# Two output gates moved between the value products of a linear attention, its heads' onsets spread, adaLN steps held around norms, context evictions moved ahead of splitting

## The chip, the cores and the metric

The kernel runs on one core of a Trainium2 chip. The metric is the time of one execution on the device, in microseconds (us); the median of three runs stands for a kernel.

## What is computed

Two transformer blocks run one after the other on 256 tokens of width 1024, in float32.

The first block has two layers. Each layer scales and shifts its input by vectors that come from a conditioning vector `c` (adaLN), runs a mixer (a bidirectional mLSTM and a dilated attention side by side), norms, and runs a SwiGLU:

```
ada = silu(c) @ w_ada[l] + b_ada[l]            # 6 vectors: sh1, sc1, g1, sh2, sc2, g2
u = h * (1 + sc1) + sh1
y = (sigmoid(g_a) * (mlstm(u) @ w_a) + sigmoid(g_b) * (attention(u) @ w_b)) @ w_out
h = layer_norm(ALPHA * h + g1 * y, ln1_g, ln1_b)
u = h * (1 + sc2) + sh2
h = layer_norm(ALPHA * h + g2 * swiglu(u), ln2_g, ln2_b)
```

The second block has two layers and a context of 256 more tokens. Layer 0 is a windowed attention with grouped keys over tokens and context, layer 1 a gated linear attention (GLA); both are followed by an MLP of width 4096 with a squared ReLU. Scales and shifts come from `silu(c) @ w_mod` in the same way, for tokens and for the context. GLA with four heads, in chunks of 64 positions and both directions, is cut to this:

```
q, k, v, out_gate = split(h @ w_in)
log_g = log_sigmoid(h @ gate_down @ gate_up + bias) / 16
b = cumsum(log_g)                       # within a chunk, and over the context
o = (tril((q*exp(b)) @ (k*exp(-b)).T)) @ v + (q*exp(b)) @ S      # S: state before the chunk
o = rms_norm(o, g_norm) * silu(out_gate)
x = x + m[2] * rms_norm(o @ w_o, g_post_mix)
```

## The kernel before, in words

**Granules.** All weights stream through the core once, as 591 granules of 512 KB (128 x 1024 floats) in one fixed list, `plan()` (line 34); 256 further granules hold the adaLN weights. A granule is named by a key such as `("gv", head, half)` or `("wo", layer, j)`. A float32 product is made of three faster matmuls: the weight is split in a high half `wh` (ACT, a rounded copy) and a low half `wl` (DVE, the difference), as the activations are, and each product is high x high, high x low, low x high.

**Ahead.** `gran(key, mm, post)` (line 483) first runs evictions that are due, then takes its granule with `G` (line 453). `G` calls `ahead(n)` (line 460), which issues the load of granule n+5 at most on SP (4 buffers `raw`), the high half of n+3 on ACT (4 buffers) and the low half of n+2 on DVE (3 buffers). So the `wl` of a granule is put into DVE's order two granules before PE uses it. Then `mm` issues the matmuls, and `post`, the eviction of the PSUM bank, is put off to the start of the next granule by `later(1, post)`. There are two PSUM buffers of name `mm`, four `aux`, two `trb`. Each engine runs its instructions in the order in which the program issues them.

**Ticks.** A granule ends with `tick()` (line 515): each generator in `self.bg` makes one step. Heads of attention, mLSTM and GLA are such generators: every step issues a few small instructions. `tick(False)` does the same without the adaLN step below. `until` and `drain` tick until a condition holds.

**adaLN steps.** `ada_step` (line 556) reduces one column block of adaLN weights against silu(c) on DVE: one pass of 128 x 1024, or two passes where tokens and context both need it (tile `junk`, then `araw`). It loads up to three blocks ahead into three `araw` buffers, counting its own. `tick` runs a step where `self.hold` is not set and the planner's lateness `nc.late` (line 372, DVE's planned time less PE's, in ns, with costs from lines 355 to 369) is below `self.room`, -250 in these stretches. `ada_need` forces the steps that are left of a vector; `affine` (line 850) needs the vectors 4 and 3 of its layer and then makes five small DVE instructions.

**layer1** (line 924) runs a layer of the first block. After the heads' projections come the branch gates `br` 0 to 7 (line 988), `wa` 0 to 7 (the products of the mLSTM's output), `wo` 0 to 7. For `wo`, `post` of an odd j makes `rT` of j-1 and j on DVE, and `trans` transposes `rT` of j-2 and j-1 on PE behind `wo` j (j even). `hold` is set after `wo` 7 and taken back at the end of `norm_to_u`. The norm is covered by filler granules of the context.

**Context.** `ctx_out` and `ctx_mlp` (lines 1727, 1758) are such fillers, in the feed-forward's end of layer 0 and of layer 1. Both use `nat` (line 1760), which multiplies two halves of four granules each and evicts two banks a half with ACT as `y` (line 1772). `relu2` and the norm's `u` and `ah` activations are on ACT too.

**GLA** (`layer2_gla`, line 1910). Granules in order: `gq`, `gg` 0 and 1 (output gates), `gdown`, four `gk`, eight `gv`, `gg` 2 to 7, then `gwo`. `decay()` runs in ticks beside `gk` and `gv`: softplus of the gate, a subtraction, and eight scans on DVE (line 1985). `head(hd, delay)` (line 2108) starts the two directions and the output of a head: exponentials on ACT, products and transposes of the decayed keys `ke`, states `gS`, the output `gon`, its norm, transposes, `go` (times the gate `og`) and the split `goT`. `bcast_cols` (line 1399) spreads a column vector over 128 rows with eight transposes into `trb` and two ACT copies.

Of the kernel before, what the change touches and what calls it, by code (L numbers as in the profile page):

```python
# [33 lines left out]
def plan():  # L34
# [95 lines left out]
    for h in range(4):  # L130
        for hf in range(2):
            g.append((("gv", h, hf), "gla_w_in_2", 0, "wsb", hf * 512, 1024 + h * 256))
    for j in range(2, 8):
        ws(("gg", j), "gla_w_in_2", 0, 2048 + j * 128)
# [242 lines left out]
class Kernel:  # L377
# [547 lines left out]
    def layer1(self, l, uT, ah, va, v1):  # L925
# [46 lines left out]
        for h in range(4):  # L972
# [13 lines left out]
            for j in range(2 * h, 2 * h + 2):  # L986
                self.gran(("o", l, j), self.mm_ws(ps[:, (j % 2) * 256:(j % 2) * 256 + 256], uT), post if j % 2 else None)
            for kind, j in EXTRA[h]:
                if l == 0 and h == 3 and (kind, j) == ("br", 6):
                    self.add(self.ctx_h())  # L990
# [28 lines left out]
        for j2 in range(4):  # L1019
            ps = self.mmb()  # L1020

            def post(j2=j2, ps=ps):
                t = self.t2("mtmp", (128, 2, 256))
                nc.vector.scalar_tensor_tensor(out=t, in0=sg(j2), scalar=1.0, in1=self.pair(ps), op0=ALU.add, op1=ALU.mult)
                nc.vector.tensor_tensor(out=t, in0=t, in1=mb.pair[j2], op=ALU.add)
                self.split(mt[j2][:, :, 0], mt[j2][:, :, 1], t)
            if j2 == 0:
                self.until(lambda: len(ydone) >= 3)
                self.first_ws([("wa", l, 0), ("wa", l, 1)], ps, lambda k: yaT[k], lambda: self.until(lambda: len(ydone) == 4))
                self.later(1, post)  # L1030
                if l:
                    self.add(self.ctx_u())
                continue
            for jj in range(2):
                self.gran(("wa", l, j2 * 2 + jj), self.mm_ws(ps[:, jj * 256:(jj + 1) * 256], yaT), post if jj == 1 else None)
# [6 lines left out]
        nc.vector.tensor_scalar(out=g1, in0=self.ada[l][:, 16:24], scalar1=0.5, scalar2=None, op0=ALU.mult)  # L1042
        cols = self.affine(l, 3, 4, (self.V(("ln1_g", l)), self.V(("ln1_b", l))))
        nat = [[None] * 2 for _ in range(2)]
# [12 lines left out]
        for j in range(8):  # L1057
# [15 lines left out]
            if j > 0 and j % 2 == 0:  # L1073
                trans(j - 2)
                trans(j - 1)
            if j == 6:
                stats(0)
# [649 lines left out]
    def ctx_out(self):  # L1727
# [3 lines left out]
        self.yc = self.halves(y)  # L1731
        yield from self.nat(lambda hf, kp: ("awo", 1, hf, kp), self.tokens(oT), self.yc, self.mmb)

# [18 lines left out]
    def ctx_mlp(self):  # L1752
        y = [self.t4("y", (128, 1024)) for _ in range(2)]
        self.yc = self.halves(y)
        yield from self.mlp_out(0, 1, self.hid_c, self.yc, self.mmb)
        self.hid_c = []
        yield from self.mlp_in(1, 1, self.uc, self.hid_c)
        self.flush()

    def nat(self, key, act, y, bank, add=False):  # L1760

        nc = self.nc
        for hf in range(2):
# [9 lines left out]
            for kp in range(4):  # L1773
                self.gran(key(hf, kp), self.mm_nat(kp, act, banks), post if kp == 3 else None)
                yield True
# [11 lines left out]

    def mlp_out(self, g, st, hid, y, bank):

        return self.nat(lambda hf, kp: ("mo", 0, g, hf, kp, st), hid if callable(hid) else self.tokens(hid), y, bank, g > 0)  # L1790

# [118 lines left out]
    def layer2_gla(self, x, xc):  # L1910
# [5 lines left out]
        for hd in range(4):  # L1916
            ps = self.mmb()
            self.grans2(("gq", hd), self.mm_ws(ps[:, 0:256], hl),
                        lambda hd=hd, ps=ps: nc.scalar.activation(out=qT[:, hd], in_=ps[:, 0:256], func=AF.Copy, scale=128 ** -0.5))
        bank = [None]  # L1920

        def gates(j0, j1, gran):

            for j in range(j0, j1):
# [4 lines left out]
                def post(j=j, ps=ps):  # L1929
                    th = self.t2("gth", (128, 2, 256))  # L1930
                    nc.scalar.activation(out=th, in_=self.pair(ps), func=AF.Tanh, scale=0.5)
                    nc.vector.scalar_tensor_tensor(out=og.pair[j // 2], in0=th, scalar=1.0, in1=self.pair(ps), op0=ALU.add, op1=ALU.mult)
                gran(("gg", j), self.mm_ws(ps[:, (j % 2) * 256:(j % 2) * 256 + 256], hl), post if j % 2 else None)
        gates(0, 2, self.grans2)
# [21 lines left out]
        def decay():  # L1956
# [33 lines left out]
            ldone.append(1)  # L1990
        self.add(decay())
        kT = [self.tv("gkT", (128, 2, 512)) for _ in range(2)]
        for hd in range(4):
            ps = self.mmb()
            self.gran(("gk", hd), self.mm_ws2(ps, h), lambda hd=hd, ps=ps: nc.scalar.activation(out=kT[hd // 2][:, hd % 2], in_=ps, func=AF.Copy))
            if hd:
                self.tick(False)
        v = [None] * 4
        ss = self.small([128, 2, 4], "gss", 1)
# [61 lines left out]
        def outputs(hd):  # L2061
# [28 lines left out]
            for jj in range(2):  # L2090
                for b in range(2):
                    nc.tensor.transpose(tr[:, jj * 256 + b * 128:jj * 256 + b * 128 + 128], on[:, b, jj * 128:(jj + 1) * 128], self.ident)
            yield
            o32 = self.t2("go32", (128, 2, 256))
            for jj in range(2):
# [17 lines left out]
        def values(hd):  # L2113
# [19 lines left out]
            for hf in range(2):  # L2133
                self.gran(("gv", hd, hf), mm(hf))
                steps(2)
        while self.adaq:
            self.ada_step()
        gmix = self.gain_cols(1, "g_post_mix_2", 2, 0)
        cols = self.scales(1, "g_pre_mlp_2", 3, 4, (0,))
        for hd in range(4):  # L2140
            if hd == 1:
                self.until(lambda: ldone)
                head(0, 1)
            if hd == 3:
                head(1, 1)
            values(hd)
        self.flush()
        head(2, 0)
        head(3, 5)
        oT = Lazy(lambda k: ot[k // 2][:, k % 2])  # L2150
        G = self.bcast_cols(gmix, "G")
        for j in range(2, 8):
            gates(j, j + 1, self.gran)
# [102 lines left out]
```

## Time and profile before

| | us |
|---|---|
| median of 3 runs (lowest, highest) | 2083.51 (2081.5, 2088.59) |
| profiled execution | 2092.44 |
| its span | 2090.7 |
| PE busy in it | 2030.9 (97%) |
| DVE, ACT busy | 1586.6 (76%), 1149.3 (55%) |
| mean DMA rate | 203 GB/s |

The span is the time from the first to the last instruction that the trace shows. PE is TensorE's matmuls, PEld its weight loads, DVE is VectorE, ACT is ScalarE, SP issues the DMAs. In a row of the timeline, the bracket gives the time for which the engine stood idle ahead of the instruction, and the instruction or transfer that ended that idle time. A weight load precedes its matmul, so the idle time of PEld is some tenths of a us longer than that of PE.

### The profile page before, as it was taken

The page shows a single profiled execution, that of the slowest core. Times are in us where ns is not written, and L with a number is a line of the kernel's source. Part 1 is how long each engine was busy: PE and PEld are TensorE (multiplying, and loading weights), DVE is VectorE, ACT ScalarE, POOL GpSimd, SP SyncE. Part 2 cuts the span into 40 slices and gives each one's busy share as a digit, 9 for nine tenths or more (in the row PEclk, how much of TensorE's full clock was granted, in tenths as well). Part 3 has the DMA queues.
Part 4 walks back from the last instruction along what each step waited for, and adds up shares of the span by engine and source line. Part 5 has one row for each costly group of instructions (what it writes and reads, how often), then busy time and mean ns, then how long its engine had stood idle before and what let it go on. Part 6 is the DMA issues. An engine that isn't in the chain of part 4 may idle for free.

```text
span 2090.7 us, 38245 instructions
## 1 busy us (share of the span) xinstructions
PE 2030.9 (97%) x15176; PEld 1888.9 (90%) x15176; DVE 1586.6 (76%) x2717; ACT 1149.3 (55%) x1968; POOL 45.1 (2%) x63
## 2 busy tenths in 40 slices
PE   7999999999999999998999999999999999999998
PEld 6999998899998989998999988899998989877997
DVE  7788988799978989988899776777563485466555
ACT  5756665655546656665744455556542464445444
POOL 0000000000000000000000000000000010000000
PEclk9999999999999999999999999999999999999999
DMA  9786566598876886555589755115553352214553
GB/s 340 281 320 213 192 235 221 187 315 305 304 254 228 284 274 233 187 202 186 167 290 358 274 196 176 61 56 176 191 183 101 115 181 75 77 65 155 188 191 132
DMA packets 120884, 426.88 MB, mean 204 GB/s; under 512 B 13664, under 2 KB 18528, under 8 KB 120704
## 3 DMA queue, kind: packets, MB, share of 16 engines
q1 hardware_dynamic: 120704, 424.43, 59.1%
q8 instruction: 119, 1.95, 0.4%
q14 instruction: 61, 0.50, 0.1%
HBM read 423.33 MB, written 1.05 MB: 203 GB/s over the span
## 4 chain that ended last, share of the span: by engine, by line
PE 87%; DVE 7%; ACT 4%; issue 1%; DMA 1%; POOL 0%; DVEq 0%; POOLq 0%; SPq 0%; ACTq 0%
PE mm L338 54%; PE aux L338 28%; PE trb L338 5%; DVE wl L338 1%; ACT wh L471 1%; DVE yg L338 1%; POOL rs L674 0%; ACT xh L1467 0%; DVE mtmp L338 0%; DMA raw<-in_w 0%; DVE xh L338 0%; DVE x L338 0%; DVE araw L338 0%; ACT ah L912 0%; DVE ee L338 0%
## 5 line engine op out<-in xcount | busy, mean ns | idle before, releaser
L338 DVE TENSOR_TENSOR wl<-raw,wh 128x1024 fp32r<-128x1024 f32 x591 | 718.7, 1221 | 153.1 <-PE aux L338 71.5
L471 ACT ACTIVATE wh<-raw 128x1024 fp32r<-128x1024 f32 x591 | 623.6, 1059 | 336.2 <-PE mm L338 117.7
L338 PE MATMUL mm<-uT,wh 128*128 128x256 f32 x3488 | 622.3, 282 | 0.0
L338 PEld LDWEIGHTS mm<-uT,wh 128*128 128x128 f32 x3488 | 531.7, 188 | 2.2 <-ACT va L814 0.3
L338 PE MATMUL mm<-uT,wl 128*128 128x256 f32 x1744 | 487.0, 279 | 0.0
L338 PE MATMUL mm<-hT,wh 128*128 128x256 f32 x1888 | 339.4, 283 | 4.8 <-ACT y L1772 2.1
L338 PEld LDWEIGHTS mm<-uT,wl 128*128 128x128 f32 x1744 | 329.6, 189 | 0.0
L338 PEld LDWEIGHTS mm<-hT,wh 128*128 128x128 f32 x1888 | 292.7, 190 | 11.5 <-ACT y L1772 2.3
L338 PE MATMUL mm<-hT,wl 128*128 128x256 f32 x944 | 265.8, 282 | 0.0
L338 DVE CUSTOM_DVE_ANT_0 araw<-araw,silu 128x1024 f32<-128x1024 f32 x192 | 233.2, 1220 | 8.4 <-DMA araw<-in_w 5.9
L338 PE MATMUL aux<-wh,hid 128*128 128x512 f32 x640 | 199.9, 394 | 0.0
L338 PEld LDWEIGHTS mm<-hT,wl 128*128 128x128 f32 x944 | 181.4, 192 | 0.0
L338 PEld LDWEIGHTS aux<-wh,hid 128*128 128x128 f32 x640 | 117.7, 188 | 23.6 <-DVE hid L338 0.2
L338 DVE TENSOR_TENSOR r<-r 128x256 f32<-128x256 f32 (+1 forms) x88 | 39.5, 448 | 117.4 <-ACT r L1905 117.3
L338 PE MATMUL aux<-mlg,wh 128*128 128x256 f32 x704 | 127.1, 283 | 0.0
L338 PE MATMUL aux<-wl,hid 128*128 128x512 f32 x320 | 124.8, 390 | 0.0
L338 PEld LDWEIGHTS aux<-mlg,wh 128*128 128x128 f32 x704 | 107.3, 188 | 0.0
L1905 ACT ACTIVATE r<-mm 128x256 f32<-128x256 f32 (+1 forms) x88 | 35.7, 406 | 125.1 <-PE mm L338 125.1
L338 PE MATMUL aux<-mlg,wl 128*128 128x256 f32 x352 | 98.8, 281 | 0.0
L674 POOL TENSOR_TENSOR rs<-ve,mhalf 128x1 f32<-128x1 f32 (+1 forms) x48 | 41.8, 871 | 2040.5 <-DVE ve L338 1853.0
L338 DVE CUSTOM_DVE_ANT_0 junk<-araw,silu 128x1024 bf16<-128x1024 f32 x64 | 77.9, 1218 | 0.0
L338 PE MATMUL mm<-wh,hT 128*128 128x256 f32 (+1 forms) x352 | 76.8, 316 | 0.6 <-DVE qs L338 0.6
(365 smaller groups left out, 3081.7 us busy)
## 6 DMA issues: line engine op xcount, KB each, us to landing
raw<-in_w SPq DMA_DIRECT2D x591, 512.0 KB, 3.9
araw<-in_w SPq DMA_DIRECT2D x192, 512.0 KB, 5.2
abias<-in_abias SPq DMA_DIRECT2D x32, 192.0 KB, 5.6
xc<-in_ctx SPq DMA_DIRECT2D x4, 512.0 KB, 6.1
x<-in_x SPq DMA_DIRECT2D x2, 512.0 KB, 4.2
gb<-in_ln SPq DMA_DIRECT2D x2, 512.0 KB, 5.4
out_x<-x SPq DMA_DIRECT2D x4, 256.0 KB, 2.0
mk<-in_mmask SPq DMA_DIRECT2D x1, 512.0 KB, 5.9
```

Source lines behind the costliest of these rows:

```text
L338: return f(*a, **k)
L471: nc.scalar.activation(out=wh, in_=self.raws[self.nhi], func=AF.Copy)
L674: nc.gpsimd.tensor_tensor(out=rs, in0=ve, in1=self.mhalf[:, 0:n], op=ALU.pow)
L1905: nc.scalar.activation(out=r[:, 0:n], in_=ps, func=AF.Relu)
```

## The change

Four parts:

1. GLA. `gg` 2 and 3 move in the plan from behind all value granules to between the two value granules of head 0 and those of head 1, each with one tick more. The heads start at other points: head 0 without delay behind the values of head 0, head 1 behind those of head 1 with a delay of 2, head 2 behind those of head 2 with 4, head 3 behind those of head 3 with 3; before, heads 0 and 1 started behind the values of heads 0 and 2 with a delay of 1, heads 2 and 3 behind those of head 3 with 0 and 5. The gain's columns and scales are made ahead of `gk`, and the broadcast `G` after the third `gk`. Four gate granules are left behind the values. A head waits for its gate before it multiplies with it (`gdone`).
2. In layer 0 and 1, `hold` is set ahead of `br` 3 of the last head. In layer 0 it is taken back after `wa` 1, in layer 1 it stays until the end of the norm.
3. `affine` of the first norm moves from ahead of `wo` 0 to behind the granule `wo` 3.
4. `nat` gets `prompt`: the eviction of a half is issued right behind the last product of that half, ahead of the next granule's splits. `ctx_out` and `ctx_mlp` use it.

```diff
@@ plan
-    for j in range(2, 8):
+        for j in (2, 3) if h == 0 else ():
+            ws(("gg", j), "gla_w_in_2", 0, 2048 + j * 128)
+    for j in range(4, 8):
         ws(("gg", j), "gla_w_in_2", 0, 2048 + j * 128)
@@ layer1
             for kind, j in EXTRA[h]:
+                if h == 3 and (kind, j) == ("br", 3):
+                    self.hold = True
...
                 if l:
                     self.add(self.ctx_u())
+                self.hold = l == 1
                 continue
...
-        cols = self.affine(l, 3, 4, (self.V(("ln1_g", l)), self.V(("ln1_b", l))))
...
                 trans(j - 1)
+            if j == 3:
+                cols = self.affine(l, 3, 4, (self.V(("ln1_g", l)), self.V(("ln1_b", l))))
@@ ctx_out, ctx_mlp: prompt=True; nat
-                self.gran(key(hf, kp), self.mm_nat(kp, act, banks), post if kp == 3 else None)
+                mm = self.mm_nat(kp, act, banks)
+                if kp == 3 and prompt:
+                    self.gran(key(hf, kp), lambda wh, wl: (mm(wh, wl), post()))
+                else:
+                    self.gran(key(hf, kp), mm, post if kp == 3 else None)
@@ layer2_gla
         self.add(decay())
+        while self.adaq:
+            self.ada_step()
+        gmix = self.gain_cols(1, "g_post_mix_2", 2, 0)
+        cols = self.scales(1, "g_pre_mlp_2", 3, 4, (0,))
...
             if hd:
                 self.tick(False)
+            if hd == 2:
+                G = self.bcast_cols(gmix, "G")
...
+            while hd not in gdone:
+                yield
             o32 = self.t2("go32", (128, 2, 256))
...
-        while self.adaq:
-            self.ada_step()
-        gmix = self.gain_cols(1, "g_post_mix_2", 2, 0)
-        cols = self.scales(1, "g_pre_mlp_2", 3, 4, (0,))
         for hd in range(4):
             if hd == 1:
                 self.until(lambda: ldone)
-                head(0, 1)
+                head(0, 0)
+            if hd == 2:
+                head(1, 2)
             if hd == 3:
-                head(1, 1)
+                head(2, 4)
             values(hd)
+            if hd == 0:
+                self.flush()
+                for j in (2, 3):
+                    gates(j, j + 1, self.gran)
+                    self.tick(False)
         self.flush()
-        head(2, 0)
-        head(3, 5)
+        head(3, 3)
         oT = Lazy(lambda k: ot[k // 2][:, k % 2])
-        G = self.bcast_cols(gmix, "G")
-        for j in range(2, 8):
+        for j in range(4, 8):
             gates(j, j + 1, self.gran)
             steps(2)
```

## Rows read from the trace of the kernel before

**Rows 1.** Page: busy share by engine; chain that ended last; adaLN's reduction group.

```profile
PE 2030.9 (97%) x15176; PEld 1888.9 (90%) x15176; DVE 1586.6 (76%) x2717; ACT 1149.3 (55%) x1968; POOL 45.1 (2%) x63
...
PE 87%; DVE 7%; ACT 4%; issue 1%; DMA 1%; POOL 0%; DVEq 0%; POOLq 0%; SPq 0%; ACTq 0%
...
L338 DVE CUSTOM_DVE_ANT_0 araw<-araw,silu 128x1024 f32<-128x1024 f32 x192 | 233.2, 1220 | 8.4 <-DMA araw<-in_w 5.9
```

**Rows 2.** Windows: us, busy time and (xinstructions) by engine, granted clock, DMA share, GB/s.

```profile
1249.00:1255.00 6.00, 4.64 (x26) 4.65 (x27) 3.22 (x5) 2.73 (x5) 0.00 (x0) 0.72 0.53 173
1776.00:1783.00 7.00, 4.15 (x22) 3.75 (x21) 4.68 (x12) 6.87 (x16) 0.00 (x0) 0.76 0.43 150
350.00:360.00 10.00, 7.60 (x67) 7.40 (x66) 8.06 (x18) 3.92 (x4) 0.00 (x0) 1.00 0.83 282
1753.85:1776.00 22.15, 22.15 (x194) 22.00 (x192) 18.62 (x22) 11.92 (x14) 0.00 (x0) 1.00 0.15 48
```

**Rows 3.** Timeline, DVE, GLA decay: start, us, engine line op, out<-in, count [idle <-releaser].

```profile
1765.83 9.03 DVE L338 TENSOR_TENSOR_SCAN ee<-reset,lg 128x512 f32<-128x512 f32 x8
1774.78 1.20 DVE L338 TENSOR_TENSOR wl<-raw,wh 128x1024 fp32r<-128x1024 f32 x1
```

**Rows 4.** Timeline, PE weight loads in GLA that waited [idle <-releaser].

```profile
1779.00 0.42 PEld L338 LDWEIGHTS trb<-ident,ke 128*128 128x128 f32 x4 [3.04 <-DVE ke L338]
...
1816.74 0.41 PEld L338 LDWEIGHTS trb<-ident,qgc 128*128 128x128 f32 x4 [1.50 <-ACT gkn L2039]
...
1818.07 0.30 PEld L338 LDWEIGHTS trb<-ident,qgc 128*128 128x128 f32 x3 [0.93 <-ACT G L1407]
...
1831.05 0.30 PEld L338 LDWEIGHTS aux<-gv,gkn 128*128 128x128 f32 x2 [1.42 <-ACT wh L471]
...
1866.08 0.30 PEld L338 LDWEIGHTS aux<-gv,ATm 128*128 128x128 f32 x2 [0.86 <-DVE ATm L338]
```

**Rows 5.** Timeline, DVE, the last head's output.

```profile
1870.37 0.42 DVE L338 COPY gon<-aux 128x256 f32<-128x256 f32 x1 [0.98 <-PE aux L338]
...
1873.28 0.62 DVE L338 TENSOR_SCALAR gon<-gon,rs 128x256 f32<-128x256 f32 x2 [0.81 <-POOL rs L674]
...
1878.77 0.69 DVE L338 TENSOR_TENSOR goT<-go,goT 128x512 fp32r<-128x512 f32 x1 [0.70 <-ACT goT L657]
```

**Rows 6.** Timeline, ACT, the last head's output.

```profile
1876.51 0.84 ACT L2096 ACTIVATE go<-trb,ggn 128x256 f32<-128x256 f32 x2 [2.36 <-PE trb L338]
1878.10 0.63 ACT L657 ACTIVATE goT<-go 128x512 fp32r<-128x512 f32 x1 [0.76 <-DVE go L338]
```

**Rows 7.** Timeline, DVE, around the output projection of layer 0.

```profile
349.10 1.22 DVE L338 CUSTOM_DVE_ANT_0 araw<-araw,silu 128x1024 f32<-128x1024 f32 x1
...
355.15 2.35 DVE L338 TENSOR_TENSOR wl<-raw,wh 128x1024 fp32r<-128x1024 f32 x2
359.37 0.88 DVE L338 SCALAR_TENSOR_TENSOR rT<-mm,g,ah 128x256 f32<-128x256 f32 x2 [1.87 <-PE mm L338]
```

**Rows 8.** Tile araw, 300 to 372 us: issue to landing of its loads.

```profile
DMA to landing us min/median/max: 3.1/4.3/8.0
```

**Rows 9.** Timeline, PE weight loads, output projection of layer 0.

```profile
353.37 0.19 PEld L338 LDWEIGHTS mm<-mT,wl 128*128 128x128 f32 x1 [2.60 <-DVE wl L338]
```

**Rows 10.** Timeline, DVE, layer 1: first pass of a double step.

```profile
944.70 1.20 DVE L338 CUSTOM_DVE_ANT_0 junk<-araw,silu 128x1024 bf16<-128x1024 f32 x1
```

**Rows 11.** Timeline, PE weight loads, layer 1.

```profile
951.23 0.14 PEld L338 LDWEIGHTS trb<-ident,mh 128*128 128x128 f32 x1 [2.11 <-ACT mh L1378]
...
977.67 0.19 PEld L338 LDWEIGHTS mm<-mT,wl 128*128 128x128 f32 x1 [2.22 <-DVE wl L338]
```

**Rows 12.** Timeline, ACT, the first eviction of ctx_mlp.

```profile
1249.70 1.09 ACT L1772 ACTIVATE y<-mm 128x512 f32<-128x512 f32 x2
```

**Rows 13.** Timeline, PE weight loads, context stages.

```profile
654.94 0.19 PEld L338 LDWEIGHTS mm<-wh,uT 128*128 128x128 f32 x1 [0.97 <-ACT y L1772]
...
1250.35 0.27 PEld L338 LDWEIGHTS mm<-hT,wh 128*128 128x128 f32 x1 [2.31 <-ACT y L1772]
```

More of the change, by code (lines that the diff above doesn't have):

```diff
@@ L1731, in ctx_out @@
         self.yc = self.halves(y)
-        yield from self.nat(lambda hf, kp: ("awo", 1, hf, kp), self.tokens(oT), self.yc, self.mmb)
+        yield from self.nat(lambda hf, kp: ("awo", 1, hf, kp), self.tokens(oT), self.yc, self.mmb, prompt=True)
     def ctx_u(self):
@@ L1754, in ctx_mlp @@
         self.yc = self.halves(y)
-        yield from self.mlp_out(0, 1, self.hid_c, self.yc, self.mmb)
+        yield from self.mlp_out(0, 1, self.hid_c, self.yc, self.mmb, True)
         self.hid_c = []
@@ L1758, in ctx_mlp, with nat @@
         self.flush()
-    def nat(self, key, act, y, bank, add=False):
+    def nat(self, key, act, y, bank, add=False, prompt=False):
         nc = self.nc
@@ L1786, in mlp_in, with mlp_out @@
             yield True
-    def mlp_out(self, g, st, hid, y, bank):
-        return self.nat(lambda hf, kp: ("mo", 0, g, hf, kp, st), hid if callable(hid) else self.tokens(hid), y, bank, g > 0)
+    def mlp_out(self, g, st, hid, y, bank, prompt=False):
+        return self.nat(lambda hf, kp: ("mo", 0, g, hf, kp, st), hid if callable(hid) else self.tokens(hid), y, bank, g > 0, prompt)
     def tokens(self, a):
@@ L1919, in layer2_gla @@
                         lambda hd=hd, ps=ps: nc.scalar.activation(out=qT[:, hd], in_=ps[:, 0:256], func=AF.Copy, scale=128 ** -0.5))
-        bank = [None]
+        bank, gdone = [None], []
         def gates(j0, j1, gran):
@@ L1932, in post @@
                     nc.vector.scalar_tensor_tensor(out=og.pair[j // 2], in0=th, scalar=1.0, in1=self.pair(ps), op0=ALU.add, op1=ALU.mult)
+                    gdone.append(j // 2)
                 gran(("gg", j), self.mm_ws(ps[:, (j % 2) * 256:(j % 2) * 256 + 256], hl), post if j % 2 else None)
```

## The prediction, before any run of the changed kernel

> **What bounds the kernel now.** I read the page first. TensorE (PE) is busy 97% of the span, and 87% of the chain that ended last is PE work, with 7% on DVE [rows 1]. The change removes no product and no pass: the same matmuls run in another order. So a part is worth only the PE idle time that it removes or makes, plus the clock that such idle time costs, and DVE, ACT and the DMA queues matter only where PE waits for them. Next I read PE's waits and weight loads, to list the gaps near the edits. The gaps that the edits can reach are 3.04 us in the gated linear attention (GLA), two at the broadcast of a gain, several under 1.5 us between its heads [rows 4], 2.60 in the output projection of layer 0 [rows 9], 2.11 and 2.22 in layer 1 [rows 11], 2.31 and 0.97 at context evictions [rows 13]. That is all there is to win: about 19 us, under 1% of the span.
>
> Two stretches carry a mean granted clock of 0.72 over 6 us and 0.76 over 7 us; a third, with an idle time as long, keeps 1.00 [rows 2]. At levels of 2.4 and 1.2 GHz the first two mean some 3.4 us at 1.2 GHz, which loses half of its work: **1.7 us**. A gap of 2.3 or 3.0 us brought this, one of 2.6 did not, so I treat the 1.7 as likely after a long gap and possible after a short one.
>
> **Part 1, GLA.** (a) Two gate granules now run between the value granules of head 0 and of head 1. PE's 3.04 us gap is a wait for decayed keys (`ke`), behind eight scans on DVE that take 9.03 us, 1765.83 to 1774.86 [rows 3, 4]. After the change these transposes come some 5.5 us later in PE's order and are not late. But the planner emits the low half `wl` two granules ahead. Today `wl` of gv(1,0) stands ahead of the scans and `wl` of gv(2,0) right behind them (1774.78, 1.20 us) [rows 3]. With two granules inserted, the one behind the scans is gv(1,0)'s own. 192 products (four value granules) take 22.15 us less a tail, 5.5 each [rows 2]. So PE reaches gv(1,0) at 1753.9 + 2 x 5.5 + 2 x 2.8 = 1770.5, or 1771.4 with the broadcast's eight transposes in front. DVE ends the scans at about 1775.8 and that `wl` at 1777.0. New gap: some 5.3 us; old gap 3.0, with the same clock slice. **+2.3**, between -1 (if the scans can start earlier) and +4. Queued behind the scans on DVE are also the gate's eviction and the next `wl`; PE then has 5.5 us of gv(1,0) to cover both.
> (b) The broadcast of the gain moves from after the value granules to the key granules, where ACT has free time. Its two gaps are 1.50 and 0.93 [rows 4]: **-2.3**.
> (c) Heads start at 0, 8, 16, 21 steps after the values of head 0, where it was 1, 13, 18, 23, with more product granules between their small steps. Six gaps stand there, the first 1.42, the last 0.86 [rows 4], 4.0 in all by PE's own starts. No row shows the new order, so I bound it from -3.6 to +1.5 and take **-1.8**, about half.
> (d) Only four gate granules (two fewer, 5.6 us) stand behind the heads, with two steps each, so head 3 finishes at its 40th step, when PE already wants its output as the fourth granule of `gwo`. The chain from output to split: 1870.37 to 1873.90, some 3.5 us [rows 5], is covered by one granule (2.8). Then transposes, the scaled eviction at 1876.51, the high half at 1878.10 [rows 6] and the low half until 1879.46 [rows 5], 2.2 to 2.95 us, with no product behind. Today two more granules cover both. **+3.7**, from 0 to +5.4 with a slice of slow clock. Part 1: **+1.9**, range -4 to +6.
>
> **Part 2, adaLN held back, layer 0.** The hold from br 3 to the second granule of `wa` skips six adaLN steps. Played through the planner's own figures, its lateness then stays above the -250 limit at each tick of wa 2 to wo 1, because the context's queue work fills DVE; one step is taken at wo 2, one at wo 3, and `affine`, moved to j = 3, then forces the other six. Gain: today two forced steps (349.10, 1.22 us each) and the affine stand ahead of two `wl` [rows 7], for which PE waits 2.60 [rows 9]; that goes, and about 0.7 in the chain of head 3: -3.3.
> Loss: what is queued behind the forced burst on DVE is `rT` of wo 2 and 3 (the eviction of j = 3 is run when wo 4 starts), and PE's transposes behind wo 4 wait for `rT`. Today PE has wo 3 done by 359.3, when that `rT` starts [rows 7]; 2.5 us earlier and with wo 4 (2.8) behind, PE asks at about 359.7. DVE is done with `wl` of wo 5 at 357.5 today [rows 7], at about 355.9 after. Seven steps at 1.15 (start to start) are 8.0, bias, affine and the first `rT` 1.2: 365.1, if no step waits, a gap of 5.4. But `araw` has three buffers and each step frees the one for the load three steps on; those loads land 3.1 to 8.0 us after issue, median 4.3 [rows 8]. With 4.1 the fourth, fifth, seventh and eighth steps end at 359.9, 362.3, 365.2 and 367.6 and the first `rT` at 368.8: a gap of **9.1 us**, bounds 5.4 and 11. I take 9.1, as these landings are in the same stretch. PE at rest that long should bring slow clock after it: +1.7, from 0 to 3.4. Layer 0: -3.3 + 9.1 + 1.7 = **+7.5**, from +2 to +11.
> Here the Trainium skill speaks against the change: "DMA: Bandwidth & Descriptors", Rules for kernel authors, says to issue a DMA early and wait for it late, so that its fixed cost overlaps; a burst over three buffers does the opposite. The page's fit (Anatomy of one DMA, made on the GpSimd path, 2.0 us + bytes / 436 GB/s) gives an estimate of 3.2 us for 512 KB, by which two rounds of waiting would be 1.8 us shorter, the gap 7.3 and the sum 1.8 us lower; the landings of this trace have a median of 4.3 and decide.
>
> **Part 3, layer 1.** Here four double steps (two passes, 944.70 being one, 1.20 each and 2.45 with overlaps [rows 10]) are held until the norm is done; nothing is forced, since layer 1's shifts were complete, and they go to the feed-forward stage, where DVE has room. The gap of 2.11 at 951.23 waits for a chain whose `mh` stood behind the step of 944.70: -1.9. The gap of 2.22 at 977.67 waits for a `wl` in a DVE queue that is 2.45 shorter: -2.2 [rows 11]. The affine's small operations before wo 0 move away: -0.5; the split of `mT` keeps its own wait: -0.3. **-4.9**, from -2.9 to -5.5. If the cover in the feed-forward stage is missing, each step costs up to 2.45 there; no PE gap in that stage waits for DVE today.
>
> **Part 4, evictions ahead of splitting.** `prompt` runs the eviction of a half right behind its last product instead of one granule later. In `ctx_mlp` the `y` copies (1249.70) stand behind four `u` activations [rows 12], and PE waits 2.31 for the banks [rows 13], with the slow slice of 1.7. Ahead of those activations the copies end before PE asks: **-3.9**, from -1 (if the next wait is the splitting itself, now 1.1 us later) to -4. In `ctx_out` the gap of 0.97 [rows 13] shrinks, but the copies go ahead of activations on which later `wl` and the norm wait: **+0.2**, from -0.7 to +1.
>
> **Sum.** 1.9 + 7.5 - 4.9 - 3.7 = **+0.8 us**. The profiled execution took 2092.4 us (span 2090.7, some 2 us around it), 9 us over the median of 2083.5; the gaps are set by order within the core, so I carry the sum over unchanged: 2093.2 for that execution, **2084.3** for the median. About 0.3%, 6.25 us, is what a measurement of this kernel can tell from no change.
>
> **Rivals.** (i) *Forecast*: layer 0 gives back what layer 1 and the context win: 2084.3, own range 2078 to 2090.
> (ii) *The burst wins, slower*: one mechanism, six forced steps behind three load buffers. If the landings are at the long end (one 8.0 us landing adds 4) and the slow clock lasts two slices (3.4), layer 0 is +12 to +13; with the tail of GLA at +5.4 the sum is +7 to +10: 2091 to 2095. It decides from a gap of about 13 us with its clock, at wo 4. For it: the median landing is already above what a gap of 9 needs. Against: SP carries fewer loads in that stretch, since weights wait too.
> (iii) *The steps do not burst, faster*: DVE reaches the burst early or its loads are ahead, so that the gap is under 3 us, and (a) is hidden: layer 0 -1, GLA -1.5, sum about -10: 2073 to 2076. For it: DVE is relieved of 6 x 1.2 = 7.2 us ahead of wo 0. Against: the planner counts PE's and DVE's time, not gaps, and by its figures starts only two.
> (iv) *It does little where it aims*: PE's next wait (the split of `mT`, the `u` activations) ends at the same time, layer 1 and the context give -3 together, and the burst is at 5.4: within 3 us of the forecast.
>
> **Chances.** Forecast 0.40, (iv) 0.17, (ii) 0.24, (iii) 0.19. The range takes in (iii)'s upper half and most of (ii): 2073 to 2095. Faster by over 0.3%: (iii) and a little of the others, 0.21. Slower: (ii) and the upper end of the forecast, 0.25. Within: 0.54.
>
> **What would show it.** Right: a new PE gap of 5 to 11 us near 360, waiting for `rT`, with eight `araw` reductions close together ahead of it and half clock behind; gaps at 353, 951, 977 and 1250 gone, 1250's slow slice too; a gap near 1772 that waits for `wl`; gaps before and inside the last granules of `gwo` waiting for `gon` and `goT`; none at the broadcast. Wrong: `araw` steps spread over wa 2 to wo 1, a gap at 360 under 4 us, no gap near 1772, or new gaps in the feed-forward stage of layer 1 behind the deferred steps. The sum hangs above all on the 9.1.

## The result, and the profile after

The changed kernel takes 2101.2 us (median of 5 runs, 2096.58 to 2102.81) against 2088.59 us for the kernel before, measured beside it again (5 runs, 2081.5 to 2090.83). The ratio is **1.0061, with a 95% interval of 1.0040 to 1.0082**: 8 to 17 us slower. The forecast was 2084.3, no change that can be told, with a range that ended at 2095. Of the 16.9 us between forecast and result, 5.1 are the base, which the forecast took from three runs (2083.51); 11.8 are the change, +12.6 where the sum said +0.8.

The page of the changed kernel, profiled execution of 2096.58 us (span 2094.8), shares of engines and the chain that ended last:

```profile
PE 2022.7 (97%) x15176; PEld 1879.4 (90%) x15176; DVE 1585.9 (76%) x2717; ACT 1149.3 (55%) x1968; POOL 45.5 (2%) x63
...
PE 85%; DVE 7%; ACT 4%; issue 2%; DMA 1%; POOL 1%; DVEq 0%; POOLq 0%; SPq 0%; ACTq 0%
```

As many products as in [rows 1], and 2 points less of the chain on PE. PE is idle 72.1 us of the span, 59.8 before: 12.3 us more. That it is busy 8.2 us less, although more of its products ran at the lower clock, goes with a faster pace of PE in this execution, to which the last section comes. The largest piece of the idle time lies where the forecast put it. DVE from wo 2 to the third `rT` of layer 0 (start, us, then the instruction; in brackets the idle time before it and what ended that):

```profile
353.02 0.87 DVE L340 SCALAR_TENSOR_TENSOR rT<-mm,g,ah 128x256 f32<-128x256 f32 x2
...
354.94 1.22 DVE L340 CUSTOM_DVE_ANT_0 araw<-araw,silu 128x1024 f32<-128x1024 f32 x1
...
357.22 1.22 DVE L340 CUSTOM_DVE_ANT_0 araw<-araw,silu 128x1024 f32<-128x1024 f32 x1
...
359.81 1.23 DVE L340 CUSTOM_DVE_ANT_0 araw<-araw,silu 128x1024 f32<-128x1024 f32 x1 [1.37 <-DMA araw<-in_w]
...
362.47 1.23 DVE L340 CUSTOM_DVE_ANT_0 araw<-araw,silu 128x1024 f32<-128x1024 f32 x1 [1.42 <-DMA araw<-in_w]
...
364.32 1.22 DVE L340 CUSTOM_DVE_ANT_0 araw<-araw,silu 128x1024 f32<-128x1024 f32 x1 [0.62 <-DMA araw<-in_w]
...
365.58 1.23 DVE L340 CUSTOM_DVE_ANT_0 araw<-araw,silu 128x1024 f32<-128x1024 f32 x1
...
368.02 1.23 DVE L340 CUSTOM_DVE_ANT_0 araw<-araw,silu 128x1024 f32<-128x1024 f32 x1 [1.20 <-DMA araw<-in_w]
...
369.24 1.23 DVE L340 CUSTOM_DVE_ANT_0 araw<-araw,silu 128x1024 f32<-128x1024 f32 x1
...
371.09 0.87 DVE L340 SCALAR_TENSOR_TENSOR rT<-mm,g,ah 128x256 f32<-128x256 f32 x2
```

One step in the tick of wo 2, one in that of wo 3, six forced, four waits for transfers that sum to 4.6 us, and behind all of it the `rT` for which PE stands. The weight loads that waited for over 1.7 us, in the whole of the changed parts:

```profile
371.62 0.28 PEld L340 LDWEIGHTS aux<-ident,rT 128*128 128x128 f32 x2 [10.87 <-DVE rT L340]
...
1054.57 0.19 PEld L340 LDWEIGHTS aux<-mlg,wh 128*128 128x128 f32 x1 [1.98 <-DVE mlg L340]
...
1769.34 0.29 PEld L340 LDWEIGHTS mm<-wl,hT 128*128 128x128 f32 x1 [4.95 <-DVE wl L340]
...
1784.74 0.73 PEld L340 LDWEIGHTS aux<-gv,gkn 128*128 128x128 f32 x4 [1.89 <-ACT gkn L2056]
...
1803.01 0.20 PEld L340 LDWEIGHTS trb<-ident,ke 128*128 128x128 f32 x2 [1.94 <-issue]
...
1850.86 0.30 PEld L340 LDWEIGHTS aux<-gv,gkn 128*128 128x128 f32 x2 [2.03 <-issue]
...
1879.94 0.14 PEld L340 LDWEIGHTS trb<-ident,gon 128*128 128x128 f32 x1 [1.75 <-DVE gon L340]
...
1883.07 0.29 PEld L340 LDWEIGHTS mm<-wh,goT 128*128 128x128 f32 x1 [2.55 <-ACT goT L659]
```

The 2.60 of [rows 9], the 2.11 and 2.22 of [rows 11], the 2.31 of [rows 13] and the broadcast's two gaps in [rows 4] are gone. The new ones are the burst's 10.87, a new one in layer 1's feed-forward stage (1054.57), and in the gated linear attention (GLA) the low half behind the scans (4.95, where [rows 4] has 3.04), a gap between the heads that waits for a copy on ACT (1.89), two more there ("issue" is time for which this view names no cause; on PE they wait for `ke` and `gS` from DVE, 1.57 and 1.66), and two at the tail. The granted clock, in windows around them (columns as in [rows 2]):

```profile
363.00:376.70 13.70, 5.08 (x24) 4.97 (x25) 9.31 (x20) 0.00 (x0) 0.00 (x0) 0.50 0.80 266
1250.00:1255.00 5.00, 5.00 (x47) 5.00 (x46) 4.54 (x7) 4.64 (x9) 0.00 (x0) 1.00 0.34 112
1766.00:1773.00 7.00, 3.66 (x18) 3.66 (x19) 6.55 (x8) 0.69 (x2) 0.00 (x0) 0.76 0.37 112
1849.00:1856.00 7.00, 5.34 (x29) 4.74 (x28) 3.92 (x8) 1.40 (x3) 0.00 (x0) 0.76 0.23 76
1880.00:1890.00 10.00, 7.68 (x22) 5.59 (x23) 3.72 (x5) 3.94 (x7) 0.00 (x0) 0.66 0.32 105
```

A mean of 0.50 is 1.2 GHz throughout: 13.7 us around the burst, of which 5.1 (371.6 to 376.7) lie behind the idle time. In GLA there are three stretches where [rows 2] has one. The context's slow stretch at 1250 is gone.

### The profile page after: what moved, and what is told of

The parts are those of the page before. It is cut to its first block, busy times and chain, and to the rows that moved or that the text cites. A ratio compares the mean times of both kernels' runs of the same rounds, so it can differ in the third digit from the quotient of the medians.

```text
span 2094.8 us, 38253 instructions
## 1 busy us (share of the span) xinstructions
PE 2022.7 (97%) x15176; PEld 1879.4 (90%) x15176; DVE 1585.9 (76%) x2717; ACT 1149.3 (55%) x1968; POOL 45.5 (2%) x63
## 4 chain that ended last, share of the span: by engine, by line
PE 85%; DVE 7%; ACT 4%; issue 2%; DMA 1%; POOL 1%; DVEq 0%; POOLq 0%; SPq 0%; ACTq 0%
PE mm L340 53%; PE aux L340 28%; PE trb L340 5%; DVE wl L340 2%; ACT wh L473 1%; POOL rs L676 1%; DVE yg L340 1%; DVE x L340 0%; DMA araw<-in_w 0%; ACT ah L914 0%; ACT xh L1473 0%; DVE ee L340 0%; DVE mtmp L340 0%; DVE xh L340 0%; DVE lnst L340 0%
## 5 line engine op out<-in xcount | busy, mean ns | idle before, releaser
L473 ACT ACTIVATE wh<-raw 128x1024 fp32r<-128x1024 f32 x591 | 623.6, 1060 | 345.4 <-PE mm L340 118.3
L340 PE MATMUL mm<-hT,wh 128*128 128x256 f32 x1888 | 332.0, 280 | 2.7 <-ACT r L1915 1.7
L340 DVE CUSTOM_DVE_ANT_0 araw<-araw,silu 128x1024 f32<-128x1024 f32 x192 | 233.3, 1220 | 11.4 <-DMA araw<-in_w 9.1
```

What stands on the lines that cost most here:

```text
L340: return f(*a, **k)
L473: nc.scalar.activation(out=wh, in_=self.raws[self.nhi], func=AF.Copy)
```

## The experiments

The first four runs do one part of the change alone each, in the kernel before; all ratios are to the kernel before.

**GLA alone**: the hunks of the diff in `plan` and `layer2_gla`, none of those in `layer1` and `nat`.

```diff
+        for j in (2, 3) if h == 0 else ():
+            ws(("gg", j), "gla_w_in_2", 0, 2048 + j * 128)
...
+                G = self.bcast_cols(gmix, "G")
...
+                head(1, 2)
```

> Only the GLA part of the change: gates, broadcast, onsets. Theory A (the trace of the changed kernel, gap by gap): the loss lies between the heads and at the tail, so this part alone costs 9 us of idle time and 2 to 3 of slow clock, +9 to +13 us over before (ratio about 1.005), with gaps of about 4.9 before gv(1,0), 8 in all between the heads, 1.5 and 2.5 in the output projection. Rival (the forecast's term): +1.9 us, no measurable difference, and the rest of the slowdown stands elsewhere.

Measured: 2105.04 us, ratio 1.0082 (1.0064 to 1.0101), +13 to +21 us. This part alone costs more than the whole change: theory A for its place, above its size. Its gaps are those of the changed kernel; what comes on top is clock. The windows of this kernel that hold slow stretches:

```profile
1770.00:1780.00 10.00, 7.18 (x38) 7.18 (x39) 7.79 (x13) 1.53 (x5) 0.00 (x0) 0.66 0.51 157
1836.00:1842.00 6.00, 5.39 (x22) 2.94 (x24) 2.94 (x5) 2.18 (x6) 0.00 (x0) 0.72 0.25 87
1856.00:1862.00 6.00, 5.14 (x27) 4.83 (x28) 2.88 (x5) 0.98 (x2) 0.00 (x0) 0.72 0.24 89
1886.00:1896.00 10.00, 7.68 (x22) 5.59 (x23) 3.72 (x5) 3.99 (x8) 0.00 (x0) 0.66 0.29 102
```

With levels of 2.4 and 1.2 GHz, these means stand for 6.8 + 3.4 + 3.4 + 6.8 = 20.4 us at the lower level; before, the same stretch has 3.4.

**Layer 0's hold and affine alone.**

```diff
+                if h == 3 and (kind, j) == ("br", 3) and l == 0:
+                    self.hold = True
...
+                self.hold = False
...
-        cols = self.affine(...)
+        if l != 0:
+            cols = self.affine(...)
...
+            if j == 3 and l == 0:
+                cols = self.affine(...)
```

> Only layer 0's part: the hold from br 3 to wa 1 and the affine behind wo 3. Theory A (trace of the changed kernel): the gap of 10.8 us at wo 4 and about 2.4 us of slow clock behind it, less 2.6 and 0.7 won, +8 to +11 us (ratio 1.004 to 1.005). Forecast's term: gap 9.1, +7.5. Rival: the burst is as long only because other parts of the change move the context's work; alone it is under +4.

Measured: 2092.4 us, ratio 1.0022 (1.0005 to 1.0040), +1 to +8 us. Its trace has the burst again, with a gap longer than in the changed kernel:

```profile
372.27 0.29 PEld L338 LDWEIGHTS aux<-ident,rT 128*128 128x128 f32 x2 [12.46 <-DVE rT L338]
```

So the gap needs no other part of the change. The time says less than the trace, and less than the 8 to 11 us of theory A: from 340 to 380 us PE is idle 13.5 us in this trace and 3.6 before, 9.9 more, and the whole part measures +1 to +8. A later section shows one thing in which executions differ; whether it explains this was not tried.

**Layer 1's hold and affine alone**: as above with l == 1, and the hold stays until the end of the norm.

```diff
+                if h == 3 and (kind, j) == ("br", 3) and l == 1:
+                    self.hold = True
...
+            if j == 3 and l == 1:
+                cols = self.affine(...)
```

> Only layer 1's part: the hold from br 3 to the end of the norm and the affine behind wo 3. Forecast's term: -4.9 us. Theory A (trace of the changed kernel): the gaps of 2.07, 2.19 and 0.40 of 0.95 go, but the deferred double steps cost 2.3 in the feed-forward stage, -2.5 to -3 us. Both are near the limit of what can be timed; the gaps at 951, 977 and in the feed-forward stage near 1050 tell them apart.

Measured: 2082.93 us, ratio 0.9981 (0.9966 to 0.9997), -0.6 to -7 us. The gaps at 951 and 977 are gone, and the deferred steps cost a new one, as in the changed kernel. Here 3.4 us of slow clock follow it (granted 0.76 from 1044 to 1051):

```profile
1044.59 0.19 PEld L338 LDWEIGHTS aux<-mlg,wh 128*128 128x128 f32 x1 [2.18 <-DVE mlg L338]
```

The time fits theory A and the forecast's term alike; the new gap is what theory A says.

**Prompt evictions alone**, in both context stages.

```diff
+                if kp == 3 and prompt:
+                    self.gran(key(hf, kp), lambda wh, wl: (mm(wh, wl), post()))
```

> Only the prompt evictions of both context stages. Forecast's term: -3.7 us, from -3.9 in the MLP (gap of 2.23 and its slow slice) and +0.2 in the attention output. Theory A (trace of the changed kernel): the same, -3.5, with the attention stage's gap of 0.70 replaced by one of 1.3 that waits for a low half. Rival: the gap at 1250 went in the changed kernel only because layer 1's hold moved the DVE work; then it stays at 2.2 here and the part is worth 0.

Measured: 2079.84 us, ratio 0.9977 (0.9959 to 0.9996), -1 to -9 us. No wait is left at 1250, so theory A holds and not its rival, while two short ones for low halves take the place of those that were won, one in each stage:

```profile
653.00 0.19 PEld L338 LDWEIGHTS mm<-wl,oT 128*128 128x128 f32 x1 [1.59 <-DVE wl L338]
...
1241.03 0.19 PEld L338 LDWEIGHTS mm<-wl,hid 128*128 128x128 f32 x1 [1.16 <-DVE wl L338]
```

One more wait went that the forecast did not list. The eviction of [rows 12] is the second of `ctx_mlp`; behind the first, PE waited in the kernel before, too:

```profile
1234.68 0.19 PEld L338 LDWEIGHTS mm<-wh,hid 128*128 128x128 f32 x1 [1.44 <-ACT y L1772]
```

The four ratios add to 1.0062 (8.2 + 2.2 - 1.9 - 2.3 thousandths), and the change measured 1.0061. The sum is known to some 3.5 thousandths only, so that it fits so closely is chance, but no effect of the parts on each other shows. Two win, two lose, and GLA decides. The next four take GLA apart.

**Only the two gates between the values.**

```diff
+        for j in (2, 3) if h == 0 else ():
+            ws(("gg", j), "gla_w_in_2", 0, 2048 + j * 128)
...
+            if hd == 0:
+                self.flush()
+                for j in (2, 3):
+                    gates(j, j + 1, self.gran)
+                    self.tick(False)
...
-        for j in range(2, 8):
+        for j in range(4, 8):
             gates(j, j + 1, self.gran)
```

> Only the two gate granules between the values of head 0 and of head 1; onsets and broadcast as before, so the heads keep their steps but four granules are left at the end. Theory A (the changed kernel's trace: a low half behind the scans, and no cover at the tail): a gap of 4.9 before gv(1,0) in place of the 3.0, the broadcast's gaps stay, the heads' gaps stay near 4, and the last head, which starts at step 23 still, ends later than the last gate, so 2.5 to 6 us of idle time at the output projection with slow clock: +6 to +10 us. Rival (the gaps between heads come from the gates' new place, since ACT then evicts a gate among the exponentials): the gaps between the heads rise to 8 here as well, +10 to +14.

Measured: 2095.48 us, ratio 1.0040 (1.0022 to 1.0057), +5 to +12 us, theory A. The low half behind the scans and the uncovered tail, and nothing new between the heads:

```profile
1770.51 0.29 PEld L340 LDWEIGHTS mm<-wl,hT 128*128 128x128 f32 x1 [4.95 <-DVE wl L340]
...
1876.50 0.14 PEld L340 LDWEIGHTS trb<-ident,gon 128*128 128x128 f32 x1 [1.33 <-DVE gon L340]
...
1879.63 0.19 PEld L340 LDWEIGHTS mm<-wh,goT 128*128 128x128 f32 x1 [2.55 <-ACT goT L659]
```

**Only the onsets.**

```diff
-                head(0, 1)
+                head(0, 0)
+            if hd == 2:
+                head(1, 2)
             if hd == 3:
-                head(1, 1)
+                head(2, 4)
             values(hd)
         self.flush()
-        head(2, 0)
-        head(3, 5)
+        head(3, 3)
```

> Only the heads' starts at 0, 8, 16, 21 steps; all six gates stay behind the values, the broadcast too. Theory A (the gaps between the heads come from the onsets: a step's transposes, its copy on ACT and the state's product fall into one granule's three ticks with no product between): the gaps between the heads rise from 4 to 8 or more with one slow slice, +4 to +7 us; two more gate granules at the end cover the tail. Rival (the gaps come from the gates in between): gaps stay at 4 or shrink, 0 to -2 us. The forecast took -1.8 for the onsets with the gates together.

Measured: 2093.76 us, ratio 1.0042 (1.0023 to 1.0061), +5 to +13 us. The weight loads between the heads that waited over 1.4 us:

```profile
1784.32 0.50 PEld L338 LDWEIGHTS aux<-gv,gkn 128*128 128x128 f32 x2 [2.24 <-ACT gkn L2040]
...
1804.40 0.31 PEld L338 LDWEIGHTS trb<-ident,ke 128*128 128x128 f32 x3 [1.94 <-issue]
...
1834.01 0.31 PEld L338 LDWEIGHTS trb<-ident,ke 128*128 128x128 f32 x3 [1.43 <-issue]
...
1856.24 0.40 PEld L338 LDWEIGHTS aux<-gv,gkn 128*128 128x128 f32 x2 [2.03 <-issue]
```

The idle time of PE itself between the first decayed keys and the last head's output sums to 7.5 us, 5.0 before (2.0 of these at the broadcast); no gate is moved in this kernel. At the tail 1.7 us for `goT` are new, too. In this execution, the slowest of eleven (2106.11), slow clock stands behind four of the gaps, 17 us in all: granted 0.66 from 1780 to 1790, and 0.76 in three windows of 7 us from 1803, 1834 and 1855. All eleven have it in part: their mean granted clock is 0.9898, against 0.9924 for the 34 of the kernel before, an estimated 5 us of work (a mean lower by 0.0026 over 2096 us), more than the 2.5 us by which the gaps grew. The fall of term (c) is the onsets'. Why the first of these gaps arises is seen on ACT, here in the changed kernel, ahead of its gap at 1784.74:

```profile
1782.20 0.60 ACT L2150 ACTIVATE gv<-mm 128x512 f32<-128x512 f32 x1 [2.23 <-PE mm L340]
1782.70 0.50 ACT L2032 ACTIVATE ke<-ee,gt 128x256 f32<-128x256 f32 x1
...
1784.11 0.58 ACT L2056 ACTIVATE gkn<-trb 128x512 f32<-128x512 f32 x1
```

PE starts the transposes of the keys at 1782.01 and has no granule to run before the product that needs their copy `gkn`. On ACT that copy stands behind the eviction of the values, which waits for the end of the granule, and behind five exponentials of the other direction. Three ticks make a granule here, and these starts put transposes, copy and product into one granule's ticks. The next gaps wait for DVE (`ke`, `gS`); how the order makes those was not followed.

**The onsets spread, at one phase of the three ticks** (starts 1, 7, 16, 22).

```diff
                 head(0, 1)
+            if hd == 2:
+                head(1, 1)
             if hd == 3:
-                head(1, 1)
+                head(2, 4)
...
-        head(2, 0)
-        head(3, 5)
+        head(3, 4)
```

> Only the heads' starts, at 1, 7, 16, 22 steps: spread as in the change, but all at the same remainder by 3 as head 0 has in the kernel before, so that transposes and the state's products fall on the same two ticks of a granule of three ticks. Theory A (the phase within a granule decides whether a product stands between transposes, copy and state's product): the gaps between the heads stay at 4 or less, -2 to +2 us, well under the kernel with starts 0, 8, 16, 21. Rival (two heads at a time are too much for ACT and DVE, whatever the phase): gaps of 7 and more, +4 to +7 as with 0, 8, 16, 21.

Measured: 2092.21 us, ratio 1.0018 (1.0000 to 1.0036), 0 to +8 us. The gaps between the heads sum to 5.6 us by the same count, with no slow stretch among them, and the mean granted clock of the twelve runs, 0.9925, is that of the kernel before. So about half of the loss goes with the phase, most of it as clock; 5.6 is more than the 4 or less that theory A named, the 1.7 us at the tail are there again, and the intervals of the two kernels overlap. That the phase is the cause is supported, not settled. For the first head it can be seen. PE starts the transposes at 1774.27 and then has a value granule to run while ACT makes the copy:

```profile
1775.89 0.77 PE L338 MATMUL mm<-wh,hT 128*128 128x256 f32 x2
...
1777.42 0.58 ACT L2040 ACTIVATE gkn<-trb 128x512 f32<-128x512 f32 x1
```

What is left between the heads is of other kinds:

```profile
1808.26 0.30 PEld L338 LDWEIGHTS aux<-gv,gkn 128*128 128x128 f32 x2 [1.72 <-ACT gsq L2083]
...
1823.95 0.30 PEld L338 LDWEIGHTS aux<-gv,ATm 128*128 128x128 f32 x2 [1.49 <-DVE ATm L338]
```

**Only the broadcast**, with the gain's columns ahead of `gk`.

```diff
+            if hd == 2:
+                G = self.bcast_cols(gmix, "G")
...
-        G = self.bcast_cols(gmix, "G")
```

> Only the gain's columns and broadcast among the key granules. Forecast and theory A: its two gaps of 1.42 and 0.85 go, -2.3 us, and no new gap near 1745 to 1760. Rival: the eight transposes and two ACT copies delay the softplus chain on ACT, and the gap of 3.0 at the first decayed keys grows by what was won: 0.

Measured: 2085.82 us, ratio 0.9983 (0.9969 to 0.9998), -0.4 to -6 us: it wins as forecast, and nothing new stands near the key granules. The three parts of GLA add to +6.5 thousandths where GLA alone has +8.2; the difference is within the intervals.

The last four look into the burst, and try what the parts point to.

**The burst without its transfers.**

```diff
...
+        if not self.fake:
+            self.ada_load(ahead)
-        self.ada_load(ahead)
...
-        g = self.adaraw.pop((w, l, v, j))
+        g = self.adaraw.pop((w, l, v, j), None)
+        g = self.old = self.old if self.fake else g
...
+            self.fake = j == 3 and l == 0
             if j == 3 and l == 0:
                 cols = self.affine(...)
```

> Layer 0's part alone, but the six forced reductions read the block of the step before once more and issue no loads, so no reduction waits for a transfer. Left out: four of the loads there, and the reductions of six column blocks of the shift of layer 0. Theory A (in the gap of 10.8 us some 4.6 are waits for transfers through three buffers, the rest is the eight passes and the order on DVE): the gap at wo 4 shrinks to about 6 us and stays, +2 to +5 us over before. Rival (transfers alone make the gap): it shrinks under 2 us, and the part gains 1 to 3 us.

Measured: 2090.0 us, ratio 1.0003 (0.9989 to 1.0016), -2 to +3 us: the gap is as theory A says, the time at or under its +2 to +5.

```profile
365.71 0.29 PEld L338 LDWEIGHTS aux<-ident,rT 128*128 128x128 f32 x2 [6.11 <-DVE rT L338]
```

The gap is 6.1 with no wait for a transfer. That is about what is left of the 10.9 in the changed kernel without its four waits of 4.6 us, and of the 12.5 in the kernel with layer 0's part alone, whose trace has four waits of 6.4. So about half of the gap is waiting for loads through three buffers, the rest is passes in DVE's order.

**The affine behind wo 3 without the hold.**

```diff
-        cols = self.affine(...)
+        if l != 0:
+            cols = self.affine(...)
...
+            if j == 3 and l == 0:
+                cols = self.affine(...)
```

> In layer 0 only the affine moves behind wo 3; no hold, so the six steps run in the ticks of br 3 to wa 1 as before and only two are left to be forced. Theory A (the hold makes the burst, the later affine alone wins): the gap of 2.56 for a low half at wo 2 goes, two forced steps (2.3 us) end before PE asks for the third rT, no gap at wo 4, -2 to -4 us. Rival (any forced step between wo 3 and its rT stops PE): a gap of 2 or more at wo 4 in place of the old one, 0.

Measured: 2086.86 us, ratio 0.9987 (0.9972 to 1.0002), -6 to 0 us. Two steps are forced, and DVE has `rT` ready in time; neither the 2.60 of [rows 9] nor a gap at wo 4 is left:

```profile
353.99 1.22 DVE L338 CUSTOM_DVE_ANT_0 araw<-araw,silu 128x1024 f32<-128x1024 f32 x1
...
355.13 1.23 DVE L338 CUSTOM_DVE_ANT_0 araw<-araw,silu 128x1024 f32<-128x1024 f32 x1
...
356.99 0.87 DVE L338 SCALAR_TENSOR_TENSOR rT<-mm,g,ah 128x256 f32<-128x256 f32 x2
```

So the hold, by making six forced steps of two, is what makes the gap in layer 0; to move the affine is harmless and probably a gain.

**The parts that win, together** (broadcast, prompt evictions, layer 1's hold, the affine behind wo 3 in both layers).

```diff
+                if h == 3 and (kind, j) == ("br", 3) and l == 1:
+                    self.hold = True
...
+            if j == 3:
+                cols = self.affine(...)
...
+                if kp == 3 and prompt:
+                    self.gran(key(hf, kp), lambda wh, wl: (mm(wh, wl), post()))
...
+            if hd == 2:
+                G = self.bcast_cols(gmix, "G")
```

> The parts that won or should win, together: gain broadcast among the key granules, prompt context evictions, layer 1's hold, the affine behind wo 3 in both layers; not layer 0's hold, the gates or the onsets. Theory A (parts add): -2.5 -4 -2.5 -3, -10 to -13 us, ratio 0.994 to 0.995. Rival (gaps removed early come back at the next wait, the pace of PE's products hides the rest): -3 or less.

Measured: **2073.78 us, ratio 0.9928 (0.9907 to 0.9948)**, -11 to -19 us. It beats both kernels. Alone, its parts were 1.7 + 2.3 + 1.9 + 1.3 = 7.2 thousandths under one, and it is 7.2 under; that sum, too, is known to some 3 thousandths. Theory A. The page has PE at

```profile
PE 2021.9 (97%) x15176; PEld 1880.6 (91%) x15176; DVE 1586.4 (76%) x2717; ACT 1149.2 (55%) x1968; POOL 45.2 (2%) x63
```

in a span of 2073.9: PE's busy time as in the changed kernel, and 20 us less idle time around it (52.0 against 72.1). Against the kernel before, 7.8 us of idle time are gone, and the mean granted clock is 0.998 in this execution (0.995 over its six) against 0.993 (0.992 over 23).

**The same, with head 0 three ticks later.**

```diff
-                head(0, 1)
+                head(0, 4)
```

> The same, and head 0 of the linear attention starts three steps (one granule of values) later, at the same remainder by 3. Theory A (the gap of 2.3 to 3.0 us at the first decayed keys is a wait behind the scans, and one more granule of values covers it): that gap goes with its slow slice, another -2 to -4 us, ratio about 0.992 to 0.993. Rival (the low half behind the scans is next, or head 0 then collides with head 1): a new gap of 1 to 3 us near, no further gain.

Measured: 2074.57 us, ratio 0.9929 (0.9911 to 0.9947). The gap at the first decayed keys is gone and no other stands in its place near it, but the time is that of the kernel above; a gain of 2 us would not show in these intervals. Inconclusive.

## Why the prediction was wrong

**What failed: part 1, term (c), the onsets.** The forecast bounded it by -3.6 and +1.5 and took -1.8, "about half" of the gaps that it saw. Alone it measures +5 to +13. The step that failed is the upper bound: it was made as if new starts could hardly add to six gaps of 1.4 us at most [rows 4], since no row showed the new order. (The 4.0 given for the six is too high as well: on PE they are 3.1 us, and 5.0 with the two of the broadcast.) The runs show 7.5 us of gaps in place of 5.0, 1.7 more at the tail, and some 5 us of lost clock. But the order could have been written out: 0, 8, 16 and 21 fall on other ticks of the three in a granule than 1, 13, 18 and 23 do, and the chain PE, ACT, PE of the first head, which has a granule of products beside it at one phase, stands bare at another. That the other gaps come of the phase as well is supported by one run, with overlapping intervals.

**What was too small: the clock.** The forecast paid 1.7 us a time, and in GLA only once, as before, with another slice at the edge of a bound. The runs show 20 us at 1.2 GHz in GLA alone where there were 3.4, and 5.1 behind the burst where 3.4 were taken. From 1740 to 1893 us PE waits 15.6 us in GLA alone and 7.8 before. The mean granted clock over all six runs is 0.988, against 0.993 over 29 of the kernel before: by an estimate from these means some 20 us more at 1.2 GHz, which lose 10 us of work. The two together, some 18, make up the +17 that was measured, though no run held the gaps and took the clock away.

**Right, by size too: (a), (d) and (b).** The low half behind the scans: gap 4.9, forecast 5.3 (its own times, 1777.0 and 1771.4, give 5.6), in place of 3.0. The tail: 1.3 and 2.55 in the kernel with the gates alone, forecast some 0.7 and 2.2 to 2.95. Together +6.0 by the forecast, measured +5 to +12, with more slow clock than it paid for. The broadcast: -2.3 forecast, -0.4 to -6.

**Right in kind: layer 0.** Two steps by ticks, six forced, `rT` behind them, four waits for transfers, all at the places named; the gap is 10.9, forecast 9.1 with bounds of 5.4 and 11. Loads took longer than the 4.1 us that was used (5.1 at the median):

```profile
DMA to landing us min/median/max: 3.5/5.1/6.3
```

The fit in "DMA: Bandwidth & Descriptors" of the Trainium skill (Anatomy of one DMA) gave an estimated 3.2 us for these loads of 512 KB. The shortest landing here, 3.5, is near that, the median is not, and the measurement decides. The rule of the same page of the Trainium skill (Rules for kernel authors), to issue a DMA early and wait for it late, agrees with the kernel without the transfers: in layer 0's part alone the gap falls from 12.5 to 6.1 us.

For layer 0's time, +7.5 was forecast and +1 to +8 measured. Why the time is near the low end although the gap is longer than forecast stays open.

**Right in sign: layer 1 and the context.** -4.9 forecast for layer 1, -0.6 to -7 measured. The two gaps went, but the cover that the forecast counted on in the feed-forward stage failed once: a deferred double step stands on DVE ahead of the split of the SwiGLU's product (`mlg`), and PE waits 2 us for that. For the context -3.7 forecast, -1 to -9 measured; both of its small new waits (1.59 and 1.16) are for a low half, the next wait that the forecast named.

**The sum.** With (c) at +8.8 (the middle of its interval) instead of -1.8, the forecast's own sum of +0.8 becomes +11.4, inside the measured 8 to 17. That this one term sets it right is partly luck: by the middles of the intervals layer 0 cost 3 us less than forecast and the two gates 2 more, the context and the broadcast won 1 more each and layer 1 won 1 less. The rival that ended slower had its mechanism at the right place, but it was not what decided: that was the term to which the text gave one sentence.

## What to carry to other kernels

When small steps of several generators are interleaved with large products, list the new order tick by tick, and look for every chain from PE over another engine back to PE that has no product between its ends; here starts that moved by some ticks cost more than the gaps that they were to hide. Before optional work is held back, look for the deadline that will call it all at once: six forced steps made a gap of 11 us here, and moving the deadline alone removed a gap and made none. Measure the parts of a bundled change apart: here two parts were worth some -4 us each, and one cost +17.

## What the runs showed of the hardware

**Two paces of PE at one granted clock.** In the feed-forward stage of layer 1 PE runs without a gap in both profiles, and yet not as fast. The same 50 us, first before, then after (columns as in [rows 2]):

```profile
1100.00:1150.00 50.00, 50.00 (x427) 50.00 (x426) 46.61 (x73) 22.55 (x30) 0.00 (x0) 1.00 0.97 357
```

```profile
1100.00:1150.00 50.00, 50.00 (x444) 50.00 (x443) 47.45 (x74) 23.28 (x31) 0.00 (x0) 1.00 0.94 345
```

427 products against 444, all of one shape (128x256), both at a granted clock of 1.00: 4% apart, 117 and 113 ns a product. The windows from 1060 to 1110 and from 1150 to 1200 have the same counts within one, so a stretch keeps one pace for over a hundred us. The profiled execution of the changed kernel wins an estimated 10 us in this way, so that it ends only 4 us behind the profiled one of before where the medians are 12.6 apart. The faster pace does not need the burst: the kernel with the two gates alone, which has no burst and is the kernel before up to GLA, has it in the same window:

```profile
1100.00:1150.00 50.00, 50.00 (x444) 50.00 (x443) 48.26 (x74) 23.37 (x31) 0.00 (x0) 1.00 0.99 378
```

The kernel without the transfers, with a gap of 6.1 at the burst, has 427 there. So equal code runs this stretch at either pace, and a difference of a few us between single profiles can be this alone. What sets the pace stays open.

**A gap's price in clock is not fixed.** The gap at the first decayed keys, 2.30 us in both kernels, came with a slow stretch in the one with layer 0's affine alone (first line), and with none in the one with the broadcast alone:

```profile
1771.00:1778.00 7.00, 4.90 (x29) 4.79 (x29) 4.69 (x10) 6.88 (x16) 0.00 (x0) 0.76 0.52 150
```

```profile
1775.00:1782.00 7.00, 4.85 (x38) 4.22 (x37) 4.68 (x12) 6.68 (x16) 0.00 (x0) 1.00 0.44 152
```

The forecast's "likely after a long gap, possible after a short one" is as far as these rows go.
